# Padding the neighbourhood scores' second matmul from 64 rows to 128

## The chip, the cores and the metric

The kernel runs on one core of one Trainium2 chip. A core has a matmul engine (PE, its weight loads shown apart as PEld), a vector engine (DVE), a scalar engine (ACT), a general engine (POOL), a queue for transfers (SP) and 16 DMA engines. The metric is the device time of one execution in microseconds, the median of the runs; lower is better.

## The reference

One layer of a diffusion backbone over 512 latent tokens of 1024 channels, with 256 context tokens. Two groups of heads, latent attention and neighbourhood attention, are followed by an output projection and a mixture of 16 experts. The part in question are the scores of the neighbourhood attention, 8 heads of 64 channels, of a row of the grid at a time:

```
s = jnp.einsum('bqhd,bjkhd->bhqjk', qr, kr).astype(jnp.float32) * scale
s = s + jnp.transpose(bias, (0, 2, 1, 3)).astype(jnp.float32)[None]
s = jnp.where(col_in[None, None, :, None, :], s, MASK_VALUE)
s_ctx = jnp.einsum('bqhd,bchd->bhqc', qr, k_ctx).astype(jnp.float32) * scale
p = jax.nn.softmax(jnp.concatenate([s, s_ctx], axis=-1), axis=-1)
```

Everything is float32.

## The kernel before

The matmul engine takes operands in a format of less precision (F32R). So a product is taken in parts: each operand is split into a high part and a low one, and the products high by high, high by low and low by high are summed. Elsewhere that is the helper `mm3` (lines 55 to 58), three matmuls. For the scores of the neighbourhood attention two are enough, because a head has 64 channels and the array 128 rows. The tile `kk` of a head holds the high part of its keys in rows 0 to 63 and the low part in rows 64 to 127. The tile `qh` holds the high part of the queries twice, in both halves. One matmul over 128 rows, L599, thus gives high by high and high by low together. The second one, L600, adds the low part of the queries by the high part of the keys, both in rows 0 to 63: it is a matmul over 64 rows.

The heads are taken in four pairs (p), each head (u) in four blocks (i) of 128 queries, 32 blocks in all. A block's scores stand in one bank of PSUM: 256 columns of keys in the window and 256 of context. For blocks 0 and 1 these are two pieces of 256 columns, for block 2 they lie side by side and are one piece of 512, for block 3 the window is in two places, so there are pieces of 128, 128 and 256. Each piece takes one L599 and one L600.

For each block the vector engine adds bias and mask (L605) and takes the row maximum (L469), ACT takes the exponential (L612), PE turns the weights (L621) a block later, and a copy takes them out of PSUM. Between the blocks PE has other work: the projections of the next pair of heads (`na_project`, through `mm3`, L56 to L58), in every second block a piece of the modulation's sums (`mod_rest`, L520), and at the change of pairs the values of the pair before (L630, L485). In the last pair the place of the projections is taken by the values of the latent attention (`mla_values`), with its weights w_ukv and w_uq. All weights of this stretch come through three staging buffers named raw, loaded by SP (L179) and cast by ACT (L554, L61). The order on each engine follows from the order of the code and a scheduler. `na_open` takes the tiles of a head from the pool `nw`, four in turn for `qh` and `ql`. `na_part` fills them.

Of the kernel before, what the change touches and what calls it, by code (L numbers as in the profile page):

```python
# [17 lines left out]
P = 128  # L18
# [12 lines left out]
# columns of the constant pack  # L31
# [6 lines left out]
def hybrid_kernel(tc, nc, x_k, x_q, ctx, cvec, w_mod_a, w_mod_b, b_mod_c, b_mod_r, g_ffn_row,  # L38
# [25 lines left out]
    # low parts that wait for their turn on the vector engine  # L64
# [22 lines left out]
    def rstd_steps(out, ss, n, n_cols, wk, first=None):  # L87
        """1 / sqrt(ss / n + eps): the root of the scalar engine, and one Newton step on its inverse.
        Of a sum in two parts the first one comes earlier."""
        v, r = (wk.tile([P, n_cols], F32, name="nw" + c, tag="nw" + c, bufs=3) for c in "vr")  # L90
        if first is None:
            roots.append(ac.activation(r, ss, AF.Sqrt, scale=1.0 / n, bias=eps).ins.name)
            ve.tensor_scalar(v, ss, -0.5 / n, -0.5 * EPS, op0=OP.mult, op1=OP.add)
        else:
            w = wk.tile([P, n_cols], F32, name="nww", tag="nww", bufs=3)
            ve.tensor_scalar(w, first, 1.0 / n, EPS, op0=OP.mult, op1=OP.add)
            ve.tensor_scalar(v, first, -0.5 / n, -0.5 * EPS, op0=OP.mult, op1=OP.add)
            ac.activation(r, ss, AF.Sqrt, scale=1.0 / n, bias=w)
            ve.scalar_tensor_tensor(v, ss, -0.5 / n, v, op0=OP.mult, op1=OP.add)
        yield  # L100
        ve.reciprocal(r, r)
        yield
        if n_cols == 1:
            ve.scalar_tensor_tensor(v, v, r, r, op0=OP.mult, op1=OP.mult)
        else:
            ve.tensor_tensor(v, v, r, op=OP.mult)
            ve.tensor_tensor(v, v, r, op=OP.mult)
        yield
        ve.scalar_tensor_tensor(out, v, 1.5, r, op0=OP.add, op1=OP.mult)
# [5 lines left out]
    # ------------------------------------------------------------ constants and small parameters  # L115
# [31 lines left out]
    # ------------------------------------------------------------ pools of the first phases  # L147
# [4 lines left out]
    # the tokens come in the places of the attentions' results  # L152
# [12 lines left out]
    # the root's table, ahead of its use  # L165
# [35 lines left out]
    def bank(*nums):  # L201
        """A bank of the sums' memory, of those named in turn."""
        n = taken[nums] = taken.get(nums, -1) + 1
        return psA.tile([P, 512], F32, name="ps", tag=f"b{nums[n % len(nums)]}", bufs=1)
# [8 lines left out]
    # ------------------------------------------------------------ modulated norm of the tokens, channel-major  # L213
# [24 lines left out]
    def mod_sums(q):  # L238
        """Shift and scale of two channel tiles, for latent and context tokens."""
# [14 lines left out]
    def mod_first(c):  # L254
        """The same of one of the first two channel tiles."""
# [90 lines left out]
    # ------------------------------------------------------------ latents of keys and values, of queries  # L346
# [30 lines left out]
    # what leaves for the memory lies apart from what follows  # L377
# [49 lines left out]
    # ------------------------------------------------------------ ring of the experts' weights  # L427
# [17 lines left out]
    def load_experts(n, behind=None):  # L445
        """Starts the loads of the next n chunks of experts' weights, in the order of their use."""
        for i in range(len(loads), min(len(loads) + n, len(order))):
# [6 lines left out]
            # few in flight, so that the small transfers between them don't queue for long  # L454
# [7 lines left out]
    # ------------------------------------------------------------ neighbourhood attention  # L462
# [3 lines left out]
    def row_max(s):  # L466
        """A block's row maximum, negated."""
# [4 lines left out]
    def softmax_block(s, pr, ssum):  # L472
        """exp of a block of scores less their row maximum, and the row sums."""
        ac.activation(pr, s, AF.Exp, bias=row_max(s), accum_out=ssum)

    def normalise_steps(ssum, wk, hi, lo):
        """Divides a pair of heads' sums by their rows' sums, which are turned into rows on the way."""
# [21 lines left out]
    # the sums of the experts' rows, by tokens  # L499
# [4 lines left out]
    # the other modulations, as rows  # L504
# [23 lines left out]

    def na_open(p):
        heads = na_heads[p] = []  # L530
        for u in range(2):
            qh = nw.tile([P, T], F32R, name="qh", tag="qh", bufs=4)
            ql = nw.tile([P, T], F32R, name="ql", tag="ql", bufs=4)
# [9 lines left out]
    def na_bias(p, u):  # L543
        """The bias of a head, with the window's mask."""
# [4 lines left out]
    def na_weights(p, j, i):  # L549
        """The high part (i = 0) and the low one (1) of the weights of queries (j = 0) or keys (1)."""  # L550
# [8 lines left out]
    def na_project(p, j):  # L559
        """Queries (j = 0), latent keys (1) or context's keys (2) of a pair of heads. Yields between the steps."""  # L560
# [9 lines left out]
    def na_part(p, j, u, i):  # L570
        """Their high part (i = 0) and low one (1), of a head."""
# [16 lines left out]
    def na_scores(p, u, i):  # L588
# [9 lines left out]
        for o, n, c in pieces:  # L598
            pe.matmul(s[:, o:o + n], qh[:, qs], kk[:, c:c + n], start=True, stop=False)  # L599
            pe.matmul(s[:, o:o + n], ql[0:64, qs], kk[0:64, c:c + n], start=False, stop=True)  # L600
# [13 lines left out]
    def na_turn(p, u, i):  # L614
        """A block's weights by keys."""
# [32 lines left out]
    # ------------------------------------------------------------ latent attention  # L648
# [9 lines left out]
    def mla_values(t):  # L658
        """Values of the latent heads, and the queries' weights and latents in two parts. Yields between the steps."""
# [29 lines left out]
    for j in range(3):  # L689
        for n, _ in enumerate(na_project(0, j)):  # L690
# [4 lines left out]
            if n == 4 and j == 1:  # L695
                na_weights(1, 0, 0)
                na_weights(1, 0, 1)
                # the table of exp, ahead of its use
# [102 lines left out]
    def halves(n):  # L801
        """Two banks for sums of 1024 columns, by halves."""
# [11 lines left out]
    def k_rope(b):  # L814
        """The part of the keys that the heads share."""
        split_later(khs[b][64:96, :], kls[b][64:96, :], krt[64:96, :])

    def queries(a, ts=range(4)):
        """Queries of four heads."""
# [18 lines left out]
    def k_prep(p, hf):  # L838
        """Keys of a pair of heads, of the latent tokens (hf = 0) or the context's (1)."""
# [39 lines left out]
    # the neighbourhood heads' part of the output projection, between the pairs  # L879
# [55 lines left out]
    def mla_turn(h, t):  # L935
        """A block's weights by keys."""
# [22 lines left out]
    def router_weights():  # L959
        """The router's sums of the second shift, the same for all rows; then its weights take up the gains of the  # L960
        second norm. Yields between the steps."""
# [88 lines left out]
    # ------------------------------------------------------------ output projection, second norm, router  # L1050
# [28 lines left out]
    def logits(ht):  # L1079
        """The router's sums for a tile's rows."""  # L1080
# [14 lines left out]
    def route(a, b):  # L1095
        """Of the tokens of tiles a to b: their two experts, and their places with them. Yields between the steps."""
# [34 lines left out]
        if b == 3:  # L1131
            # what the last tile's tokens have before them
# [15 lines left out]
    def shares():  # L1148
        """Of all tokens: the weights of their experts, in two parts."""
# [17 lines left out]
        # the rows of the sums: a token's, less its place and the rows of the tokens  # L1167
# [5 lines left out]
    def places(oh, a, b, base, n_rows, a0=0):  # L1173
        """Ones where a token's place is one of those from base on."""
# [5 lines left out]
    def slot_sums(pq, oh, va, i, n_i, n_rows):  # L1180
        """Sums over the tokens of a place: the row it reads (i = 0); its weight and the row it adds to (i = 1)."""
# [7 lines left out]
    def slot_gains(pq, idx_, wsl_, n_rows):  # L1189
# [3 lines left out]
        # places without a token add to rows of their own, past those of the tokens  # L1193
# [15 lines left out]
    def rows_half(t, hf):  # L1209
        """Half of the columns of a tile's residual sum, their squares' sum, and they times the gain."""  # L1210
# [48 lines left out]
    # the last tile's steps between those of the tiles before it  # L1259
# [67 lines left out]
    # ------------------------------------------------------------ experts  # L1327
# [14 lines left out]
    def weights(q, fine=False, wh=None):  # L1342
        """A chunk of weights in two parts, of which the low one takes the place of the chunk before."""
# [19 lines left out]
    def spare(shape, dt=F32, lent=False, at=None):  # L1363
        """A slot of the ring, for other ends: for good, or until the next load."""
# [4 lines left out]
    # the places past the first ones, where an expert has them  # L1369
    NB = -(-(T - CAP) // P)  # L1370

    def overflow():
# [8 lines left out]
        # rows, and later the sums of them  # L1381
# [104 lines left out]
    # what waits for the parts of the next chunks, of the one behind them  # L1486
# [14 lines left out]
    def turn_second(hf):  # L1501
        """Half of the channels of the second expert's rows, in the place of the first one's."""
# [18 lines left out]
    def load_next(q):  # L1521
        """Loads in the places that the chunks up to q leave."""
# [5 lines left out]
    def front(e, q, ws):  # L1528
        """A part of the sums of an expert's two factors."""
# [23 lines left out]
    def back(e, q, ws):  # L1553
        """A part of the sums over an expert's products."""
# [7 lines left out]
    def put():  # L1562
        """The last sums of an expert's rows, to the places of their tokens."""
# [20 lines left out]
    with tc.manual_schedule(engines={pe.engine, ve.engine, ac.engine}):  # L1584
        # the table of the gate's function, ahead of its use
# [26 lines left out]
    # ------------------------------------------------------------ the last experts, sum of all and last norm  # L1612
    # their rows go to the tokens on the tensor engine, the others' went by way of memory
# [18 lines left out]
    def direct(u, i, t, hf, stop=False):  # L1632
        """Adds a part of a direct expert's rows to a tile's tokens."""
# [4 lines left out]
    with tc.manual_schedule(engines={pe.engine, ve.engine, ac.engine}):  # L1638
# [11 lines left out]
        def half(i, ahead=LA):  # L1650
            """Half i of the last chunks; those behind it are parted ahead of what waits for its sums."""
# [32 lines left out]
        # the root's table, ahead of its use  # L1684
# [139 lines left out]
def _layout(**n):  # L1824
# [11 lines left out]
    # per quarter of the channels: pairs of row tiles, of each the columns of the shift and of the scale  # L1836
    wa = wm[:, :2048].reshape(4, 2, P, 2, 4, 256).transpose(4, 0, 2, 1, 3, 5)
    # of the first quarter a channel tile at a time
# [3 lines left out]
    # per quarter, in the order (shift or scale, channel tile, token kind); then the gains  # L1842
# [55 lines left out]
```

## Time and profile before

| | us |
|---|---|
| median of 3 runs | 760.02 (759.91 to 760.87) |
| profiled execution, first to last instruction (span) | 759.4 |
| PE busy | 721.5 (95%) |
| DVE busy | 546.4 (72%) |
| ACT busy | 446.0 (59%) |
| POOL busy | 77.8 (10%) |

The page gives no other time of the profiled execution than its span. The median lies 0.6 us above it. A matmul's busy time is modelled to its end and overlaps that of the next one, so the distance between starts tells what a matmul costs, not its duration. Names stand for program tiles: out<-in. A form like 64*128 is rows by columns of the stationary operand.

### The profile page before, as it was taken

To read this page: it belongs to the slowest core of one execution; us is meant where nothing else is said; L and a number is where in the kernel's file an instruction comes from. 1 tells how busy PE (TensorE), PEld (TensorE's weight loads), DVE (VectorE), ACT (ScalarE), POOL (GpSimd) and SP (SyncE) were. 2 spreads that over 40 slices of the span, in tenths; PEclk is the share of its full clock that TensorE was granted. 3 is DMA by queue.
4 is the path that set the end of the run, shared out by engine and by line. 5 is a ranking of instruction groups with operands and counts; after the bars stand their busy time and mean duration, and the time that the engine had idled before them with its cause. 6 is when DMAs were issued, how large, how long until landed. Compare 5 with 4: busy or idle time off the path is not lost. (4 is left out here: it accounts for less than half of the span.)

```text
span 759.4 us, 10561 instructions
## 1 busy us (share of the span) xinstructions
PE 721.5 (95%) x3982; PEld 527.0 (69%) x3983; DVE 546.4 (72%) x744; ACT 446.0 (59%) x697; POOL 77.8 (10%) x46
## 2 busy tenths in 40 slices
PE   4999999999999999999999929999999999999995
PEld 4679987666665588776666826777777777777773
DVE  5572465646565589474564758999999999999996
ACT  6452364444434466464583428777777777777773
POOL 1000000000000000000000001033222322221220
PEclk9999999999999999999999958999999999999998
DMA  8931237544446662031139968999999999999872
GB/s 324 406 99 49 83 131 244 187 146 146 140 140 220 182 227 85 28 112 42 43 144 345 339 231 309 351 377 371 356 361 367 368 354 359 364 355 384 309 131 110
DMA packets 39621, 176.94 MB, mean 233 GB/s; under 512 B 5288, under 2 KB 6768, under 8 KB 27280
## 3 DMA queue, kind: packets, MB, share of 16 engines
q1 hardware_dynamic: 35168, 164.24, 58.6%
q0 software_dynamic: 4112, 11.92, 7.4%
q8 instruction: 32, 0.52, 0.3%
q14 instruction: 21, 0.17, 0.1%
q10 hardware_dynamic: 288, 0.08, 0.0%
HBM read 163.00 MB, written 15.32 MB: 235 GB/s over the span
## 5 line engine op out<-in xcount | busy, mean ns | idle before, releaser
L1356 DVE TENSOR_TENSOR el<-ew,eh 128x2048 fp32r<-128x2048 f32 (+1 forms) x106 | 220.5, 2087 | 20.7 <-ACT eh L1353 13.4
L1353 ACT CAST eh<-ew 128x1024 fp32r<-128x1024 f32 x190 | 189.7, 1048 | 43.2 <-PE s L58 28.6
L56 PE MATMUL s<-eh,xh 128*96 128x512 f32 x260 | 104.4, 401 | 0.9 <-ACT xh L61 0.9
L58 PE MATMUL s<-eh,xl 128*96 128x512 f32 x260 | 102.8, 396 | 0.0
L57 PE MATMUL s<-el,xh 128*96 128x512 f32 x260 | 102.4, 394 | 0.0
L1567 POOL DMA_INDIRECT ya_d<-yo,idx x14 | 45.5, 3253 | 140.4 <-DVE yo L1571 140.4
L58 PEld LDWEIGHTS s<-eh,xl 128*96 128x96 f32 x260 | 42.2, 162 | 19.1 <-DVE xl L62 0.6
L56 PEld LDWEIGHTS s<-eh,xh 128*96 128x96 f32 x260 | 42.2, 162 | 17.9 <-ACT xh L61 1.2
L57 PEld LDWEIGHTS s<-el,xh 128*96 128x96 f32 x260 | 42.3, 163 | 17.3 <-DVE el L1356 0.2
L56 PE MATMUL y<-eh,ghh 128*96 128x512 f32 x120 | 48.2, 401 | 0.0
L58 PE MATMUL y<-eh,ghl 128*96 128x512 f32 x120 | 47.3, 394 | 0.0
L57 PE MATMUL y<-el,ghh 128*96 128x512 f32 x120 | 47.2, 393 | 0.0
L56 PE MATMUL ps<-wh,hh 128*128 128x512 f32 (+2 forms) x128 | 43.8, 345 | 0.4 <-ACT hh L274 0.3
L469 DVE TENSOR_REDUCE nm<-s 128x1 f32<-128x768 f32 x32 | 30.5, 954 | 19.0 <-PE s L58 18.7
L58 PE MATMUL ps<-wh,hl 128*128 128x512 f32 (+2 forms) x128 | 43.5, 345 | 0.3 <-DVE hl L276 0.3
L57 PE MATMUL ps<-wl,hh 128*128 128x512 f32 (+2 forms) x128 | 43.3, 341 | 0.0
L1284 POOL MEMSET xg<- 128x1024 f32 x2 | 1.8, 950 | 388.0 <-DMA g<-mod_d 388.0
L605 DVE TENSOR_TENSOR ps<-ps,bb 128x256 f32<-128x256 f32 x32 | 13.8, 432 | 35.1 <-PE ps L600 35.0
L56 PE MATMUL ps<-hh,wh 128*128 128x512 f32 (+1 forms) x96 | 38.7, 403 | 0.0
L1242 POOL DMA_INDIRECT xg<-hx_d,idx x16 | 23.6, 1475 | 118.9 <-DVE va L1165 50.5
L933 ACT ACTIVATE pr<-s,nm 128x768 f32<-128x768 f32 x32 | 29.0, 908 | 9.6 <-DVE nm L469 9.3
L58 PE MATMUL ps<-hh,wl 128*128 128x512 f32 (+1 forms) x96 | 34.5, 359 | 0.0
(357 smaller groups left out, 1501.4 us busy)
## 6 DMA issues: line engine op xcount, KB each, us to landing
ew<-w_gate SPq DMA_DIRECT2D x32, 1024.0 KB, 9.3
ew<-w_up SPq DMA_DIRECT2D x32, 1024.0 KB, 9.2
ew<-w_down SPq DMA_DIRECT2D x32, 1024.0 KB, 9.3
raw<-w_mod_b SPq DMA_DIRECT2D x32, 512.0 KB, 3.8
wm<-w_mod_a SPq DMA_DIRECT2D x16, 512.0 KB, 9.2
raw<-w_qk SPq DMA_DIRECT2D x8, 512.0 KB
ya_d<-zero SPq DMA_DIRECT2D x10, 256.0 KB, 7.5
raw<-w_v SPq DMA_DIRECT2D x4, 512.0 KB
```

Of the source, the lines that this page charges most:

```text
L56: pe.matmul(ps, lh, rh, start=start, stop=False)
L57: pe.matmul(ps, lh, rl, start=False, stop=False)
L58: pe.matmul(ps, ll, rh, start=False, stop=stop)
L469: ve.tensor_reduce(out=nm, in_=s, axis=AX.X, op=OP.max, negate=True)
L605: ve.tensor_tensor(s[:, 0:256], s[:, 0:256], bb[:, 1 if i == 3 else 0, :], op=OP.add)
L933: ac.activation(pr, s, AF.Exp, bias=nm, accum_out=mla_ssum[h // 2][:, t, h % 2:h % 2 + 1])
L1242: ins = gp.indirect_dma_start(out=xg[e % NX][slice(0, CAP), :], out_offset=None, in_=hx_d, in_offset=bass.IndirectOffsetOnAxis(ap=idx[slic ...
L1284: gp.memset(x_, 0.0)
L1353: ac.copy(wh[:, cs], r[:, cs])
L1356: ve.tensor_tensor(wl[:, cs], r[:, cs], f(wh[:, cs]), op=OP.subtract)
L1567: gp.indirect_dma_start(out=ya_d, out_offset=bass.IndirectOffsetOnAxis(ap=idx[rows, 1, e:e + 1], axis=0), in_=yo[rows, :], in_offset=None, ...
```

## The change

The low part of the queries gets four tiles of its own, taken in turn as before. Their lower halves (rows 64 to 127) are set to zero once, by POOL. L600 then runs over all 128 rows: the added rows multiply zeros with the low part of the keys. The number of matmuls and their columns stay. (The diff's other hunks empty lines of comment only. Line 599 and 600 become 603 and 604, and 605 becomes 609.)

```
+    qls = [nw.tile([P, T], F32R, name=f"ql{n}") for n in range(4)]
+    for ql in qls:
+        gp.memset(f(ql[64:128, :]), 0.0)
+
     def na_open(p):
         heads = na_heads[p] = []
         for u in range(2):
             qh = nw.tile([P, T], F32R, name="qh", tag="qh", bufs=4)
-            ql = nw.tile([P, T], F32R, name="ql", tag="ql", bufs=4)
+            ql = qls[(2 * p + u) % 4]
...
             pe.matmul(s[:, o:o + n], qh[:, qs], kk[:, c:c + n], start=True, stop=False)
-            pe.matmul(s[:, o:o + n], ql[0:64, qs], kk[0:64, c:c + n], start=False, stop=True)
+            pe.matmul(s[:, o:o + n], ql[:, qs], kk[:, c:c + n], start=False, stop=True)
```

On PE, at the scores of a block of two pieces with a projection behind it, stands before (kk are the keys, qh and ql the queries, hh and hl the tokens, wh and wl the projection's weights):

```order
L599 MATMUL ps<-kk,qh 128x256
L600 MATMUL ps<-kk,ql 128x256
L599 MATMUL ps<-kk,qh 128x256
L600 MATMUL ps<-kk,ql 128x256
L56 MATMUL ps<-hh,wh 128x512
L57 MATMUL ps<-hl,wh 128x512
```

In the same place stands now:

```order
L603 MATMUL ps<-kk,qh 128x256
L604 MATMUL ps<-kk,ql_1126 128x256
L603 MATMUL ps<-kk,qh 128x256
L604 MATMUL ps<-kk,ql_1126 128x256
L56 MATMUL ps<-hh,wh 128x512
L57 MATMUL ps<-hl,wh 128x512
```

Nothing moved on PE. Only the tile's name is new: it is one of four fixed ones.

On POOL, between the loads of small parameters at the start and the first memset of the experts' stage, stands now, with what each waits for:

```order
L144 DMA wr<-w_r 128x160
L145 DMA brb<-b_r 128x20
L531 MEMSET ql_1125 64x512 [waits DMAHW6_49,DMAHW4_49,DMAHW7_49,DMAHW2_49,PE_49]
L531 MEMSET ql_1126 64x512
L531 MEMSET ql_1127 64x512 [waits DMAHW5_49,DMAHW0_49,PE_49]
L531 MEMSET ql_1128 64x512
L1288 MEMSET xg_4121 128x1024 [waits DMAHW3_49,DMAHW2_49,DMAHW4_49,DMAHW1_49,DMAHW5_49,DMAHW0_49,DMAHW6_49,DVE_49,DMAHW7_49,PE_49,Pool_49]
```

The four memsets of L531 are new; the rest stood there before in the same order.

## Rows read from the trace of the kernel before

**Rows 1.** Busy time by engine in two stretches, with PE's granted clock
```profile
118.00:262.00 144.00, 144.00 (x800) 91.77 (x800) 81.67 (x143) 65.61 (x136) 0.00 (x0) 1.00 0.52 171
452.00:742.00 290.00, 287.26 (x1353) 203.94 (x1353) 270.67 (x183) 218.51 (x245) 71.70 (x33) 0.99 0.96 335
```
**Rows 2.** Waits, 118 to 262 us: total, times, longest
```profile
DVE ps L605 <- PE ps L600: 35.0, 24, 3.4
...
PEld ps L600 <- issue: 7.4, 27, 0.8
...
PEld ps L520 <- DMA raw<-w_mod_b: 0.3, 1, 0.3
```
**Rows 3.** Line L600: ns least, median, most; first and last start; forms
```profile
L600 PE MATMUL ps<-kk,ql x64: 322/380/502, 123.2 to 254.0; 64*128 64x256 f32 x40, 64*128 64x128 f32 x16, 64*128 64x512 f32 x8
```
**Rows 4.** In order of time on PE, a block 0: start, us, what
```profile
137.93 0.28 PE L599 MATMUL ps<-kk,qh 128*128 128x256 f32 x1
138.14 0.38 PE L600 MATMUL ps<-kk,ql 64*128 64x256 f32 x1
138.45 0.39 PE L599 MATMUL ps<-kk,qh 128*128 128x256 f32 x1
138.77 0.38 PE L600 MATMUL ps<-kk,ql 64*128 64x256 f32 x1
139.08 0.50 PE L56 MATMUL ps<-hh,wh 128*128 128x512 f32 x1
139.41 0.40 PE L57 MATMUL ps<-hl,wh 128*128 128x512 f32 x1
```
**Rows 5.** In order of time on PE, a block 2
```profile
165.63 0.40 PE L599 MATMUL ps<-kk,qh 128*128 128x512 f32 x1
...
166.72 0.39 PE L57 MATMUL ps<-hl,wh 128*128 128x512 f32 x1
166.95 0.39 PE L58 MATMUL ps<-hh,wl 128*128 128x512 f32 x1
167.18 0.60 PE L621 MATMUL ps<-c,pr 128*128 128x128 f32 x4
```
**Rows 6.** In order of time on PE, a block 3
```profile
132.58 0.22 PE L599 MATMUL ps<-kk,qh 128*128 128x128 f32 x1
...
134.45 0.39 PE L57 MATMUL ps<-hl,wh 128*128 128x512 f32 x1
```
**Rows 7.** In order of time on PE, projection of 256 columns
```profile
118.08 0.28 PE L58 MATMUL ps<-hh,wl 128*128 128x256 f32 x1
118.20 0.28 PE L56 MATMUL ps<-hh,wh 128*128 128x256 f32 x1
```
**Rows 8.** In order of time on PE, from 96 rows to 128
```profile
290.51 0.28 PE L58 MATMUL s<-kh,ql 96*128 96x256 f32 x1
290.63 0.40 PE L56 MATMUL x<-wh,onh 128*128 128x512 f32 x1
```
**Rows 9.** In order of time, weight loads, behind the block 0 above
```profile
139.18 0.19 PEld L57 LDWEIGHTS ps<-hl,wh 128*128 128x128 f32 x1
```
**Rows 10.** Lines L1284 and L245
```profile
L1284 POOL MEMSET xg<- x2: 948/950/953, 392.2 to 393.1; 128x1024 f32 x2
...
L245 PE MATMUL ps<-wm,sstat x192: 272/273/297, 25.2 to 46.8; 128*32 128x128 f32 x192
```
**Rows 11.** In order of time on ACT, exponential of the block before rows 5
```profile
163.63 0.69 ACT L612 ACTIVATE pr<-ps,nm 128x512 f32<-128x512 f32 x1
```
**Rows 12.** In order of time, w_ukv from load to use
```profile
218.90 0.38 SPq L179 DMA_DIRECT2D raw<-w_ukv  x1
...
225.62 0.62 ACT L61 CAST wh<-raw 128x512 fp32r<-128x512 f32 x1 [2.30 <-DMA raw<-w_ukv]
...
226.66 0.50 PE L56 MATMUL ps<-wh,kvh 128*128 128x512 f32 x1
```
**Rows 13.** In order of time on PE, at the lower clock
```profile
458.22 0.63 PE L57 MATMUL s<-el,xh 128*96 128x512 f32 x1
```

## The prediction

> **What bounds the kernel now.** I read the share of each stretch first, then the waits, then the matmuls one by one in order of time. The change touches only the neighbourhood attention, whose scores run from 123 to 254 us. In 118 to 262 us the matmul engine (PE) is busy 144.00 of 144 us at the full granted clock of 1.00 (2.4 GHz), the vector engine (DVE) 81.67 and the scalar engine (ACT) 65.61 [rows 1]. So PE should bound this stretch, and the waits say the same: the other engines wait for PE (35.0 us in 24 waits on the second matmul of the scores alone), while PE waits for data almost never, 0.3 us once for a weight load. One row of that view is odd: 7.4 us in 27 times in which the weight loads (PEld) of L600 stood idle without a releaser, "issue" [rows 2]. A busy PE is not an effective one, so the start times decide.
>
> In order of time the reader sees the cost. A matmul of 128 rows and 256 columns behind its like starts 0.12 us after it [rows 7], one of 512 columns 0.23 us [rows 5]. In the block of rows 4 the four score matmuls of 256 columns start 0.21, 0.31, 0.32 and 0.31 us apart, and the projection L56 behind them takes 0.33 us to the next start instead of 0.23. L600 uses 64 rows, its neighbours 128. Every change from 128 rows to 64 or back exposes a weight load of about 0.1 to 0.2 us: the matmul can't overlap its predecessor. A change from 96 rows to 128 costs nothing: 290.51 to 290.63 is 0.12 us [rows 8]. So it is the 64-row form that costs, not the mere difference in rows.
>
> **What the change removes.** There are 64 L600 in 32 score blocks: 40 of 256 columns, 16 of 128, 8 of 512 [rows 3]. Padded to 128 rows, every matmul of a block has the form of its neighbours. Time from a block's first L599 to the second matmul behind the block, now and after, with 0.12 for up to 256 columns and 0.23 for 512:
> - Blocks 0 and 1 of each head, 16 in all, two pieces of 256: now 139.41 - 137.93 = 1.48 us [rows 4]; then 4 x 0.12 + 0.23 = 0.71. Saved 0.77, in all 12.3 us.
> - Block 2, eight in all, one piece of 512: now 166.72 - 165.63 = 1.09 [rows 5]; then 3 x 0.23 = 0.69. Saved 0.40, in all 3.2 us.
> - Block 3, eight in all, pieces of 128, 128 and 256: now 134.45 - 132.58 = 1.87 [rows 6]; then 6 x 0.12 + 0.23 = 0.95. Saved 0.92, in all 7.4 us.
> Together 22.9 us. In the order of the instructions eight blocks are followed by transposes and one by the values' matmul of 64 columns, where I expect only part of the follower's share back: minus 0.5, an estimate. That leaves 22.4 us. No row shows the padded L600 itself. From below its spacing is the 0.12 us of rows 7; from above it is the 0.31 us of today [rows 4], with no gain. I take the near end, because the padded matmul has exactly the shape of the rows it is taken from. The 64 rows of zeros add no columns, and columns set the spacing.
>
> **What it adds.** Four memsets of 64 x 512 on POOL. The only like row is 0.95 us for 128 x 1024 [rows 10], so about 0.48 us each, 1.9 us together. They wait for places that the modulation's matmuls L245 leave, the last of which starts at 46.8 us [rows 10], and for their loads. POOL has nothing to do then, the next thing in its queue is a memset at 392 us, and the first padded matmul comes at 123 us. Cost 0; if they held up the vector engine for all of their length and that reached the end, 1.9 us. The first padded matmuls also wait for POOL's semaphore, long since up. PE, DVE, ACT and SP keep their order, and the query tiles rotate as before.
>
> **What is late next.** PE becomes faster than what feeds it, so I looked for the slack of each wait. The exponentials have much: in block 2 of rows 5 the transposes L621 start at 167.18, and their exponential ends at 163.63 + 0.69 = 164.32 [rows 11], 2.9 us earlier. One block gives back at most 0.92 us, and the exponential itself moves up with the scores of its own block. In the first three pairs of heads I expect no new wait.
>
> The last pair is different: its eight blocks share three staging buffers ("raw") between the modulation's weights and the latent attention's weights. The load of w_ukv is issued at 218.90, when the buffer is free, and is cast by ACT from 225.62 to 226.24; ACT already waits for it. PE uses the cast at 226.66, 0.42 us later [rows 12]. Between the matmul that frees the buffer and this use stand one block of each kind, 0.40 + 0.92 + 0.77 = 2.09 us saved, so PE will wait about 2.09 - 0.42 = 1.7 us. The other loads of that pair have under a microsecond to spare, and one is late already by 0.3 us [rows 2]. I take 1.4 us more for them: an estimate between 0 and 4.0, what is left of the eight blocks' 4 x 0.77 + 2 x 0.40 + 2 x 0.92 = 5.7 us.
>
> Behind 262 us nothing is tied to an absolute time: the experts' loads start when buffers come free. From 452 to 742 us PE is busy 287.26 of 290 us and the DMA share is 0.96 [rows 1]. Both move up together, so the saving arrives whole.
>
> **The sum.** 22.4 - 1.7 - 1.4 = 19.3 us. The profiled execution has a span of 759.4 us, from which the stretch would end 19.3 us earlier, at 740.1. The median of the runs is 0.6 us above that span; I keep the difference: 760.0 - 19.3 = 740.7 us.
>
> **The rivals.**
> - Nothing new is late: the loads of the last pair arrive earlier because PE frees the buffers earlier. Then all of 22.4 to 22.9 us stays: about 737.4 us. For it: PE alone frees most of the buffers. Against it: the ACT row that already waits for w_ukv.
> - Loads bind in all pairs. Sixteen times PE multiplies two half-megabyte loads of modulation weights. At half a microsecond of wait each time 8 us are gone beside the 3.1 above, and the gain is 11.3: 748.7 us. For it: three buffers, and the stretch then moves the same bytes in 13% less time. Against it: a DMA share of 0.52 [rows 1], and a single late weight load so far [rows 2].
> - The weight load stays exposed. Were the overlap lost because L599 and L600 share array rows, padding would remove nothing, L600 would stay 0.31 us behind L599, and the time would be 760.0. Against it: the load of L57 starts at 139.18 [rows 9], while L56, with all 128 rows in common, runs from 139.08 for 0.50 us [rows 4]. The Trainium skill, page "TensorE: Matmul & The Clock Gate", Part 3, "What overlaps and what doesn't", says that a weight load overlaps a running matmul only where their row groups differ. By that sentence the change would bring nothing; the trace does not bear it out for these matmuls.
> - Slower: PE's new wait at the start of the last pair lets its clock fall. At the lower clock of 1.2 GHz a matmul of 512 columns shows 0.63 us, where it shows 0.39 at full clock [rows 13, 5]. If the remaining 26 us of the stretch ran at half clock and PE stayed the bound, they would cost up to 26 us more: 766.7. It decides where a wait at the handover grows to several microseconds. Against it: the waits worked out are 1.7 us and less, and the stretch holds 1.00 now.
>
> **How the numbers follow.** My forecast, 738.5 to 744 us, gets 0.65. Nothing new late: 0.13. Loads bind more widely, 744 to 753 us: 0.15. Exposed load, no gain: 0.04. Lower clock, slower: 0.03. From 736.8 to 747.0 us lie the first two and about a third of the third, a little over 0.8. A measurement of this kernel tells about 0.2%, 1.5 us, from no change. Faster than that: 0.65 + 0.13 + 0.15 = 0.93; within it 0.04; slower 0.03.
>
> **What would show it.** In the profile after: the second score matmul in the form 128*128, its mean near 0.28 us for 256 columns instead of 0.38, starts 0.12 us apart within a block, no "issue" idle before its weight load. Block 0 to the second projection behind it in 0.7 us. The stretch that ended at 262 us ends near 243. New waits of PE for ACT's cast of w_ukv, 1 to 2 us, and for raw in the last pair. From there to the end the same length. I am wrong if the starts stay 0.3 us apart, if PE waits for raw in the first three pairs, or if the stage is shorter and the end is not.

## The result, and the profile after

| | median us | runs (lowest to highest) | ratio to before, 95% interval |
|---|---|---|---|
| before | 759.96 | 4 (759.78 to 760.87) | |
| after | 742.27 | 4 (738.56 to 742.79) | 0.9759 [0.9736, 0.9782] |

The change takes 17.7 us off the median; 19.3 were forecast. The profiled execution of after took 742.79 us with a span of 740.6, 18.8 less than the span before.

First the shares, as in [rows 1], for after and in two parts: up to the last pair of heads, and the last pair.

```profile
core 0: us, PE busy (x) PEld busy (x) DVE busy (x) ACT busy (x) POOL busy (x), PEclk, DMA share, GB/s
118.00:205.00 87.00, 87.00 (x587) 64.95 (x589) 56.12 (x100) 45.02 (x94) 0.00 (x0) 1.00 0.58 189
205.00:244.00 39.00, 36.29 (x227) 22.39 (x220) 24.04 (x42) 19.36 (x40) 0.00 (x0) 0.96 0.61 199
```

For three pairs PE is as full as before and its clock is full. In the last pair it has gaps of 2.7 us, and its clock falls for a while. The waits of that stretch (118 to 244 us; total, times, longest), beside [rows 2]:

```profile
DVE ps L609 <- PE ps L604: 18.9, 11, 2.5
...
ACT wh L61 <- DMA raw<-w_ukv: 3.0, 1, 3.0
...
PEld ps L520 <- DMA raw<-w_mod_b: 2.5, 5, 1.0
...
PE ps L56 <- ACT wh L61: 1.7, 1, 1.7
...
PEld ps L604 <- issue: 0.8, 1, 0.8
...
PE ps L520 <- DMA raw<-w_mod_b: 0.9, 2, 0.6
```

DVE's wait for the second matmul fell from 35.0 us to 18.9, and the "issue" idle of its weight load from 27 times to one. In their place stand waits for loads, all in the last pair. New are those of PE: 1.7 us for ACT's cast of w_ukv (L61) and 0.9 for w_mod_b. ACT's wait for w_ukv was there before (2.3 us, [rows 12]) and is 3.0 now, and the wait of L520's weight load for w_mod_b grew from 0.3 us to 2.5. The second matmul by itself, against [rows 3]:

```profile
L604 PE MATMUL ps<-kk,ql x64: 273/281/496, 120.5 to 233.3; 128*128 128x256 f32 x40, 128*128 128x128 f32 x16, 128*128 128x512 f32 x8
```

Its form is 128*128 and its median 281 ns instead of 380. The same three blocks as in [rows 6, 4, 5], in order of time on PE (start, us, what): of the block 3 the first and the last row, then the block 0, then the block 2.

```profile
128.13 0.22 PE L603 MATMUL ps<-kk,qh 128*128 128x128 f32 x1
...
129.04 0.39 PE L57 MATMUL ps<-hl,wh 128*128 128x512 f32 x1
...
132.52 0.28 PE L603 MATMUL ps<-kk,qh 128*128 128x256 f32 x1
132.63 0.27 PE L604 MATMUL ps<-kk,ql 128*128 128x256 f32 x1
132.75 0.28 PE L603 MATMUL ps<-kk,qh 128*128 128x256 f32 x1
132.86 0.28 PE L604 MATMUL ps<-kk,ql 128*128 128x256 f32 x1
132.98 0.40 PE L56 MATMUL ps<-hh,wh 128*128 128x512 f32 x1
133.21 0.40 PE L57 MATMUL ps<-hl,wh 128*128 128x512 f32 x1
...
155.78 0.39 PE L603 MATMUL ps<-kk,qh 128*128 128x512 f32 x1
...
156.48 0.40 PE L57 MATMUL ps<-hl,wh 128*128 128x512 f32 x1
```

From first row to last these take 0.91, 0.69 and 0.70 us; the forecast said 0.95, 0.71 and 0.69, and before it was 1.87, 1.48 and 1.09. So the core of the forecast holds matmul by matmul. The handover to the last pair, in order of time on PE (in square brackets the idle time before an instruction, and what ended it):

```profile
206.18 0.28 PE L604 MATMUL ps<-kk,ql 128*128 128x256 f32 x1
208.17 0.50 PE L56 MATMUL ps<-wh,kvh 128*128 128x512 f32 x1 [1.72 <-ACT wh L61]
208.60 1.07 PE L634 MATMUL ps<-pt,nav 128*64 128x512 f32 x2
209.60 0.68 PE L57 MATMUL ps<-wl,kvh 128*128 128x512 f32 x1
210.08 1.06 PE L625 MATMUL ps<-c,pr 128*128 128x128 f32 x4
210.79 0.78 PE L58 MATMUL ps<-wh,kvo 128*128 128x512 f32 x1
211.36 0.41 PE L603 MATMUL ps<-kk,qh 128*128 128x256 f32 x1
211.58 0.42 PE L604 MATMUL ps<-kk,ql 128*128 128x256 f32 x1
```

PE waits 1.72 us for ACT's cast of w_ukv, where 1.7 was worked out. From 209.8 us on, its clock shows the lower level, 1.2 GHz, for 3.4 us (columns as in the first view, PEclk 0.53):

```profile
209.60:213.20 3.60, 3.60 (x16) 2.98 (x16) 1.62 (x5) 2.03 (x5) 0.00 (x0) 0.53 0.52 190
```

In that stretch L625's four transposes take 1.06 us instead of the 0.60 of [rows 5], and L603 and L604 start 0.22 us apart instead of 0.12. That was in the forecast only as the unlikely rival.

Where the 18.8 us of the spans came from is read from the start of the same PE instruction in both traces (before minus after):

| place | ahead by, us | step, us |
|---|---|---|
| before the first score matmul | 2.6 | +2.6 |
| second L604 of the last pair's first block | 20.2 | +17.6 |
| after the wait for w_ukv | 18.5 | -1.7 |
| end of the neighbourhood stage, after a late w_mod_b | 20.1 | +1.6 |
| router | 18.0 | -2.1 |
| last matmul | 18.4 | +0.4 |

The change itself explains the steps from 2.6 to 20.1, which are 17.5 us. The first 2.6 come before anything of the change runs. The same work in order of time on PE, first in before:

```profile
13.43 1.97 PE L224 MATMUL ps<-c,xb 128*128 128x128 f32 x8 [1.82 <-DVE nwv L93]
15.33 1.06 PE L260 MATMUL ps<-wm,sstat 128*32 128x128 f32 x10
```

and in after:

```profile
13.53 1.10 PE L224 MATMUL ps<-c,xb 128*128 128x128 f32 x8 [1.64 <-DVE nwv L93]
14.61 0.62 PE L260 MATMUL ps<-wm,sstat 128*32 128x128 f32 x10
```

Both start within 0.1 us of each other, but eight transposes take 1.97 us in one and 1.10 in the other. The trace's first record of PE's clock at full speed stands at 19.4 us in before and at 11.8 in after. The loss at the router is one row of after's waits from 395 to 440 us, which before did not have:

```profile
DVE t L1223 <- DMA hx_d<-t: 2.8, 1, 2.8
```

DVE waits there for the store of an earlier tile's rows. Whether these two belong to the change is asked below.

### The profile page after: what moved, and what is told of

Read it like the earlier page. It is cut to its first block, busy times and chain, and to the rows that moved or that the text cites. A ratio compares the mean times of both kernels' runs of the same rounds, so it can differ in the third digit from the quotient of the medians.

```text
span 740.6 us, 10570 instructions
## 1 busy us (share of the span) xinstructions
PE 699.0 (94%) x3982; PEld 521.0 (70%) x3983; DVE 545.6 (74%) x744; ACT 445.9 (60%) x697; POOL 79.6 (11%) x50
## 5 line engine op out<-in xcount | busy, mean ns | idle before, releaser
L469 DVE TENSOR_REDUCE nm<-s 128x1 f32<-128x768 f32 x32 | 30.5, 954 | 19.4 <-PE s L58 19.2
L56 PE MATMUL ps<-hh,wh 128*128 128x512 f32 (+1 forms) x96 | 36.4, 380 | 0.0
L57 PE MATMUL ps<-hl,wh 128*128 128x512 f32 (+1 forms) x96 | 34.2, 356 | 0.0
```

The costliest lines, as they stand in the source:

```text
L56: pe.matmul(ps, lh, rh, start=start, stop=False)
L57: pe.matmul(ps, lh, rl, start=False, stop=False)
L469: ve.tensor_reduce(out=nm, in_=s, axis=AX.X, op=OP.max, negate=True)
```

## The experiments

The experiments ran in two groups, each on one chip beside runs of before: e1 to e4 (before: median 759.53 us, 17 runs) and e5 to e8 (759.72, 7 runs).

**e1: the kernel after, unchanged, once more.**

> The changed kernel once more, to see how its time spreads and whether its waits come back. If the wait for w_ukv at the handover to the last pair (1.7 us) and the fall of the clock behind it (3.4 us at half clock) belong to the kernel, the profile shows both again and the median lies at 741.5 to 743 us. If the fall of the clock is chance, it is missing in this profile, and the times lie near 740.

Measured: 739.73 us (6 runs), ratio 0.9750 [0.9721, 0.9779]. The wait for w_ukv came back with 1.6 us on PE, and so did the lower clock behind it, from 209.7 us for 3.4 us. DVE's wait for hx_d is not in this trace. The median is below what I expected of it: the gain here is 19.8 us where the first comparison gave 17.7. So what is the same from run to run is the stage; the router's 2 us are not.

**e2: the fixed tiles and the memsets, but 64 rows as before.**

```
-            pe.matmul(s[:, o:o + n], ql[:, qs], kk[:, c:c + n], start=False, stop=True)
+            pe.matmul(s[:, o:o + n], ql[0:64, qs], kk[0:64, c:c + n], start=False, stop=True)
```

> The four fixed query tiles and their memsets stay, but the second matmul runs over 64 rows again. Theory (changes between the 64-row and the 128-row form expose weight loads): no gain, 759 to 761 us, L604 back at 0.31 us to the next start. Rival (the gain comes from where the tiles lie or from the fixed tiles): 742 us.

Measured: 759.29 us (10 runs), ratio 1.0002 [0.9981, 1.0023]. The second matmul and the waits read as before the change (line, ns least, median, most; then idle before its weight load):

```profile
L604 PE MATMUL ps<-kk,ql x64: 322/380/500, 120.4 to 251.3; 64*128 64x256 f32 x40, 64*128 64x128 f32 x16, 64*128 64x512 f32 x8
its engine sat idle before it (us, times) until:
  issue: 7.4, 27
```

The tiles that no longer rotate and the four memsets are worth nothing either way; all of the gain is in the form of the matmul. This trace also settles the start: its clock rose at 11.9 us, its span is 756.9 us, and its kernel is no faster than before. So the first 2.6 us in the comparison of spans are not the change's.

**e3: 96 rows instead of 128.**

```
-            pe.matmul(s[:, o:o + n], ql[:, qs], kk[:, c:c + n], start=False, stop=True)
+            pe.matmul(s[:, o:o + n], ql[0:96, qs], kk[0:96, c:c + n], start=False, stop=True)
```

> The second matmul runs over 96 rows instead of 128. Theory in the form that 64 rows are another form of the array and 96 are not (rows 8): as with 128 rows, 741 to 743 us, starts 0.12 us apart. Rival (any difference in rows between neighbours exposes the load): about 760 us, starts 0.3 us apart.

Measured: 741.02 us (4 runs), ratio 0.9753 [0.9722, 0.9783], the same as after's.

```profile
L604 PE MATMUL ps<-kk,ql x64: 273/283/499, 120.4 to 234.5; 96*128 96x256 f32 x40, 96*128 96x128 f32 x16, 96*128 96x512 f32 x8
```

96 rows among matmuls of 128 behave as 128 do. So it isn't that the rows must be equal: 96 and 128 get on, 64 and 128 don't, as [rows 8] had it.

**e4: before, with the matmuls of a block in another order: all first ones, then all second ones, of 64 rows.** The flags that start and end a sum go with the new order.

```
         for o, n, c in pieces:
-            pe.matmul(s[:, o:o + n], qh[:, qs], kk[:, c:c + n], start=True, stop=False)
-            pe.matmul(s[:, o:o + n], ql[0:64, qs], kk[0:64, c:c + n], start=False, stop=True)
+            pe.matmul(s[:, o:o + n], qh[:, qs], kk[:, c:c + n], start=(o == 0), stop=False)
+        for o, n, c in pieces:
+            pe.matmul(s[:, o:o + n], ql[0:64, qs], kk[0:64, c:c + n], start=False, stop=(o + n == 512))
```

> The kernel before, with 64 rows, but in each block all first matmuls stand ahead of all second ones, so blocks 0 and 1 change form twice instead of four times, block 3 twice instead of six times. Theory (the price is per change of form): block 0 from 1.48 to 0.12 + 0.21 + 0.12 + 0.31 + 0.33 = 1.09 us, 16 times 0.39; block 3 from 1.87 to 0.12 + 0.12 + 0.21 + 0.12 + 0.12 + 0.31 + 0.33 = 1.33, 8 times 0.54; 10.5 us in all, less about 1 of new waits in the last pair: 750 to 752 us. Rival (a matmul of 64 rows is slow by itself, whatever stands beside it): 759 to 761 us.

Measured: 750.78 us (4 runs), ratio 0.9871 [0.9837, 0.9906]. In order of time on PE, two blocks one behind the other (start, us; x2 is two matmuls):

```profile
122.57 0.28 PE L599 MATMUL ps<-kk,qh 128*128 128x256 f32 x1
122.78 0.50 PE L601 MATMUL ps<-kk,ql 64*128 64x256 f32 x2
123.21 0.50 PE L599 MATMUL ps<-kk,qh 128*128 128x256 f32 x2
123.64 0.50 PE L601 MATMUL ps<-kk,ql 64*128 64x256 f32 x2
124.07 0.50 PE L56 MATMUL ps<-hh,wh 128*128 128x512 f32 x1
124.41 0.39 PE L57 MATMUL ps<-hl,wh 128*128 128x512 f32 x1
```

Each group of two takes 0.43 us to the next start, but not as 0.12 and 0.31, as the expectation had it. One by one the starts are 122.57, 122.78, 123.00, 123.21, 123.43, 123.64, 123.87 and 124.07: about 0.21 us each, across a change of form as well as inside a group. So a change lengthens the distance that it falls in by about 0.1 us and the next one by as much. In [rows 4] each distance behind the first has a change in it and one just before it, which gives the 0.31. The weight loads show the same: in after the load of L604 starts with the matmul before it (132.52 us), 0.11 us ahead of its own; in e4 the load of the first matmul behind a change starts only with its own matmul (122.78 and 123.21 us), and that of the second again 0.11 ahead (122.89). The 64-row matmuls are as many as before; only the changes are fewer, two in a block instead of two for each second matmul (64 in all instead of 128). Of e1's 19.8 us 8.7 come with half of the changes. So the price hangs on the change from one form to the other, about 0.19 us in all between matmuls of 256 columns, and not on the 64-row matmul as such.

**e5: after, with four staging buffers instead of three.** To make room, the unused results of the square sums lie in tiles that are free then, the zeros for the experts' sums are one tile of 64 columns that is read eight times, and q1 and q2 have one buffer each.

```
-        return chp.tile([P, 1024], F32, name="raw", tag="raw", bufs=3)
+        return chp.tile([P, 1024], F32, name="raw", tag="raw", bufs=4)
```

> The changed kernel with four staging buffers raw instead of three (for the room the square sums' junk goes to places not yet or no longer in use, the zeros are 64 columns wide and read repeatedly, two small tiles have one buffer). Theory (what the last pair of heads loses are late loads behind the three buffers, and the clock falls because PE idles at the handover): the waits of PE for ACT's cast of w_ukv (1.7 us) and for w_mod_b (about 0.9) go, the clock stays at full in the stretch, 0.8 us, so 3 to 3.5 us less than e8: 736 to 738 us. Rival (the loads take their time whatever the number of buffers): the waits stay, same as e8 within a microsecond.

Measured: 736.75 us (4 runs), ratio 0.9703 [0.9677, 0.9729]. The last pair in e5, as in the first view above:

```profile
core 0: us, PE busy (x) PEld busy (x) DVE busy (x) ACT busy (x) POOL busy (x), PEclk, DMA share, GB/s
205.00:244.00 39.00, 38.39 (x257) 25.68 (x257) 25.79 (x46) 22.37 (x47) 0.00 (x0) 1.00 0.73 247
```

PE is busy 38.39 of 39 us against 36.29 in after and 36.11 in e8, at full clock. PE's wait for the cast of w_ukv is gone; ACT still waits 1.2 us for a load of w_ukv, which no longer reaches PE. The gain over e8, the kernel after on the same chip, is 4.1 us by the medians; the two ratios' intervals overlap, so its size is known only roughly, a little more than I expected. The DMA share of that stretch rises to 0.73 (0.63 in e8): there was room on the queues.

Its make-up is another than I expected. From the first score matmul to the last values' matmuls (L634) PE takes 118.98 us in e8 and 114.84 in e5. Of these 4.1 us 2.3 are PE's idle time (2.9 us in e8, 0.6 in e5). The clock gives nothing here, since it did not fall in e8 either. The rest, 1.9 us, comes with a new order on PE: the modulation's matmuls (L520, form 128*32) between the handover and these values' matmuls stand in four groups of eight in e5, and in e8 in one of eight and six of four. No run has the fourth buffer without the new order and the smaller tiles, so what each is worth by itself is not shown.

**e6 and e7: the stores of hx_d through POOL's queue instead of SP's**, on top of e5 (e6) and of after (e7).

```
-        return sy.dma_start(hx_d[t * P:(t + 1) * P, :], h2s[t]).ins.name
+        return gp.dma_start(hx_d[t * P:(t + 1) * P, :], h2s[t]).ins.name
```

> As e5, and the stores of the normed tokens hx_d go out by POOL's queue instead of SP's, where they stood behind the experts' loads. Theory (the vector engine waits for a store of hx_d in some runs, 2.8 us in the profile after, because the store stands behind loads): that wait is gone, the gathers of the experts' rows come earlier, 1 to 3 us less than e5. Rival (the store and the gather are slow because the DMA engines are full): no difference from e5, or some microseconds more because POOL issues the stores slower.

> The changed kernel with the stores of hx_d on POOL's queue alone. Theory: 1 to 3 us less than e8, 738 to 740 us; rival: as e8, or more.

Measured: e6 736.54 us, ratio 0.9694 [0.9672, 0.9716], no difference from e5; e7 741.22 us, ratio 0.9746 [0.9723, 0.9769], no difference from e8. My theory, that the stores are late because they stand behind other transfers in SP's queue and that this costs time, fell. In e5 the router's stage has two waits for hx_d:

```profile
PE t L1503 <- DMA xg<-hx_d,idx: 5.8, 1, 5.8
...
DVE t L1224 <- DMA hx_d<-t: 2.0, 1, 2.0
```

In e6 DVE's is gone, and PE's for the gathered rows, which follow the stores, is longer:

```profile
PE t L1503 <- DMA xg<-hx_d,idx: 7.5, 1, 7.5
```

So the end stays. That the wait only moved from DVE to PE is not shown: PE's wait for the gathered rows differs as much between traces that keep SP's queue (5.7 us in e8, 8.0 in e3). DVE's wait for the store is 2.8 us in after, 2.0 in e5, 1.2 in e2, which has no gain, and absent in e1, e3 and e8. It comes and goes with the same kernel, and so I don't count it to the change; what decides it from run to run was not found.

**e8: the kernel after, on the chip of e5 to e7.**

> The changed kernel once more, beside the three others on the same chip: 740 to 742.5 us.

Measured: 740.90 us (4 runs), ratio 0.9738 [0.9697, 0.9778]. The handover in e8, to be laid beside that of after:

```profile
207.52 0.28 PE L604 MATMUL ps<-kk,ql 128*128 128x256 f32 x1
209.40 0.50 PE L56 MATMUL ps<-wh,kvh 128*128 128x512 f32 x1 [1.60 <-ACT wh L61]
209.82 1.07 PE L634 MATMUL ps<-pt,nav 128*64 128x512 f32 x2
210.83 0.50 PE L57 MATMUL ps<-wl,kvh 128*128 128x512 f32 x1
211.16 0.60 PE L625 MATMUL ps<-c,pr 128*128 128x128 f32 x4
211.52 0.47 PE L58 MATMUL ps<-wh,kvo 128*128 128x512 f32 x1
211.83 0.28 PE L603 MATMUL ps<-kk,qh 128*128 128x256 f32 x1
211.95 0.28 PE L604 MATMUL ps<-kk,ql 128*128 128x256 f32 x1
```

The wait is there, 1.60 us, and the clock does not fall (PEclk 1.00):

```profile
209.60:213.20 3.60, 3.60 (x19) 2.07 (x19) 2.80 (x7) 2.44 (x6) 0.00 (x0) 1.00 0.88 343
```

L625 takes 0.60 us, the scores start 0.12 apart. The wait belongs to the kernel; the lower clock followed it in after, e1 and e3, and not in e7 and e8. In the three the clock had first risen at 11.7 to 12.0 us, in the two at 16.7 and 17.5. In e6, where the wait is gone, it rose at 11.9 and did not fall; nor did it fall there in before, e2, e4 and e5, where PE waits at most 0.3 us for this cast. So in these traces the fall comes only with the wait, and the start seems to decide whether it follows; five traces don't prove the second. Its price is read from the two traces of the same kernel: from the wait to the end of the stage e8 wins 2.9 us on before, after wins 1.6, so the fall costs about 1.3 us where it comes. That is net: PE's waits for w_mod_b are 0.4 us shorter in after (0.9 against 1.3), so the lower clock by itself took about 1.7.

## Why the prediction was right, point by point

**The mechanism.** Right. PE bounded the stage, and a change between the 64-row form and the 128-row form was what cost. e2 (same tiles, old form, no gain), e3 (96 rows, full gain) and e4 (old form, half the changes, 8.7 of 19.8 us) rule out the other causes that were named: the tiles' places, unequal rows as such, and a 64-row matmul that is slow by itself. The rival that the weight load stays exposed anyway is out. It was the one that spoke against the change: by the Trainium skill, page "TensorE: Matmul & The Clock Gate", Part 3, "What overlaps and what doesn't", L604 would have stayed about 0.31 us behind L603; the trace shows 0.12, with all row groups in common.

**What it removes: 22.9 less 0.5.** Right to 3%, 21.8 for 22.4. From the first block to the handover 17.6 us were measured. By the forecast's terms these are 12 blocks at 0.77, 6 at 0.40, 6 at 0.92 and the last pair's first block, 17.9 before the follower's deduction. The last pair's other seven blocks were forecast at 5.0 us; in e8, where the clock holds, the blocks there win about 4.2 (the 2.9 above and 1.3 of PE's waits for w_mod_b). So the blocks gave 21.8 us, and the follower's deduction from 22.9 is 1.1 us rather than 0.5: that term was a little too small.

**What it adds.** The cost of 0 is right (e2), the size a little off. The four memsets of after (ns least, median, most; first and last start):

```profile
L531 POOL MEMSET ql<- x4: 517/544/667, 43.0 to 44.5; 64x512 f32 x4
```

They take some 0.54 us each instead of 0.48 and end long before the first use at 120.5 us.

**The new wait.** Right: 1.72 us in after, 1.6 in e1, e7 and e8, 1.8 in e3, for 1.7. Slack against saving was enough to find it, since the load itself takes about as long as before: 6.72 us from issue to cast in [rows 12], 6.98 in after (200.52 to 207.50).

**Other raw loads, 1.4 us.** The place was right, and so was the size: PE's waits for w_mod_b are 0.9 us in after, and 1.1, 1.9, 1.2 and 1.3 in e1, e3, e7 and e8. That is partly luck, for the 1.4 was only put somewhere between 0 and 4.0. In the first three pairs no wait of PE for raw came, which was the doubt behind the rival with 748.7 us.

**The clock.** The sum had nothing for it. The rival had the mechanism right (PE's wait at the handover, then the lower level), but its condition, a wait of several microseconds, was wrong: 1.7 us was enough in three traces out of five of kernels with three buffers. It was held only 3.4 us, not for the rest of the stretch (which was about 33 us from there to the forecast's own end at 243, not 26), so it cost about 1.3 us and could not turn the sign.

**Behind the stage.** "The saving arrives whole" is right but for the router's stage: some 2 us were lost there in after's profile, none in e1's. With the forecast's 19.3 us stand 17.7, 19.8 and 18.8 in three comparisons of the same pair of kernels. The profile of before was one in which the clock rose late at the start, and that of after one with the late store: their spans agree with the forecast better than their parts do, since the two nearly cancel. That is luck. The sum also kept 0.6 us between span and median. In every execution whose time and span are both on record the time lies 1.7 to 3.3 us above its own span, so the profiled execution of before took at least some 761 us by this estimate, and the 0.6 was no property of the kernel.

## What to carry to other kernels

On PE look at the start-to-start time of neighbours, not at the busy share: this stage was busy 144 of 144 us and 21.8 us of it were changes of form. Where a few 64-row matmuls stand among 128-row ones, try padding them with zeros (here to 96 or 128 rows, 19.8 us), and if that can't be, grouping them (here 8.7 us), since the price is paid at each change. When the engine that sets the pace gets faster, compare the saving between two uses of each buffer with the load's slack: here that named the next wait to within 0.1 us, and one more staging buffer, with the order on PE that came with it, brought another 4 us (736.75).

## What the runs showed of the hardware that I had not expected

- A wait of 1.6 to 1.8 us on an otherwise full PE was followed by 3.4 us at the lower clock in after, e1 and e3, and by nothing in e7 and e8, where the wait was as long.
- The clock's first rise varies between executions (19.4 us in before's profile, 17.5 in e7, 16.7 in e8, 11.7 to 11.9 in after, e1 and e2). Measured against before, it moves the first score matmul forward by 0.8 us in e7 and by 2.6 to 2.8 in after, e1 and e2. Spans of two single profiles are therefore compared only from a common point on.
- One change between a 64-row and a 128-row matmul is paid in two places, about 0.1 us in the distance that it falls in and as much in the next one (e4).
